# One decoder layer on one core: the first projection's four units side by side by k tiles, constant matmuls in front, a later memory norm and a reordered last product

## The chip, the cores and the metric

The kernel runs on one core of a Trainium2 chip. The metric is the device time of one execution in microseconds. Lower is better. An execution is profiled as well; its trace gives the span from the first to the last instruction and the times of every instruction.

## The reference, cut to what matters

A hybrid decoder layer over 512 positions of width 1024, all in float32:

```
h = rms_norm(x, norm_mix)
hq, hf, hi, hg, mq, mk, mv = split(h @ w_in)          # 4 x 512 and 3 x 512 columns
f = lb + (1 - lb) * sigmoid(hf)                       # HGRN2: q, f, input, gate
x = x + concat(hgrn2(hq, f, hi, hg), moba(mq, mk, mv)) @ w_out
x = x + cross_attention(rms_norm(x, norm_xattn), rms_norm(mem, norm_mem), ...)
x = x + square(relu(rms_norm(x, norm_mlp) @ w_ff1)) @ w_ff2
return rms_norm(x, norm_final)
```

The first projection of this text is `hf`: four heads of 128 columns, contracted over 1024 rows. The memory is `mem`, 256 tokens of width 1024, with a norm of its own (`rstd` is the reciprocal root of its mean square). The last product is the one with `w_ff2`, followed by the residual add and the final norm.

## The kernel before, in words

Every activation is kept transposed, features on the 128 partitions and positions along the free dimension. A contraction over 1024 is eight k tiles of 128. Each float32 operand is split into a high part (rounded to the fp32r type by ScalarE, tile `wh` or `xhi`) and a low part (the remainder, by VectorE, `wl` or `xlo`), and a product is three fp32r matmuls: high by high, high by low, low by high.

Weights come in units of 128 x 1024 float32 (512 KB). A unit is loaded by an SP DMA into a raw tile (`load_unit`, three buffers), split by `split_unit`, and used by the matmuls of `fm_k` or `tm_stage`. `need(u)` is called ahead of unit u and loads up to 6 units and splits up to 2 units ahead of it. Instructions of the head of the kernel and of the MLP run in the order in which the program writes them (`manual_schedule`); each engine works through its own queue in that order.

**The head.** `load_x(k)` loads the eight 256 KB tiles of x, `split_x(k)` splits each with the norm's gain, `square_x(k)` squares it (even k on ScalarE, odd k on VectorE) and VectorE adds the squares to `Sx` and `Sy`. Units 0 to 3 hold one head of `hf` each, all eight k tiles of it side by side. Units 0 and 1 are loaded and split in two parts. The matmuls run for heads 0 and 1 together, k by k, then head 2, then head 3: 4 x 8 x 3 = 96 matmuls of 128 x 512. At `NORM_AT`, behind head 2's k = 6, stand two matmuls with a tile of ones (`nr`) that sum `Sx` over the partitions; ScalarE makes `rb1`, the reciprocal root, out of them (`rsqrt_of`: Ln, then Exp). `ev_f` multiplies the four results by `rb1`. The next stage is `hi` (a `tm_stage`).

**Side work.** Chains of small steps (generators) are put between the matmuls by `pump`. A planner (`Pace`) keeps a model time for each engine; a chain that yields a list of tiles goes on when the model has them ready, and one that yields a number goes on that many model microseconds later. `mem_prep` is such a chain: it loads and splits the memory, sums its squares and calls `norm_rows`, which issues the `nr` matmuls, Ln and Exp (`rbm`), and then transposes `rbm` into a column with small matmuls against the identity (`nc`, result `rcm`). It runs inside the `wo` stage.

**The tail.** The last product runs in seven passes of eight steps (`PLAN`; a step i is one weight unit, 8 k tiles with one 512-column matmul by the high part and one 256-column matmul by the low part). In steps 52 to 55 the outputs are taken in the order `LAST` = 0, 2, 1, 3, and right behind each step's matmuls `ends_last` adds both 256-column halves of the accumulator to the residual (two VectorE adds) and calls `norm_part` (square, scaled copy, sum). `final_half(nb)` sums the squares over partitions with float32 matmuls against ones, takes the reciprocal root, multiplies the half's output in four VectorE pieces and issues one output DMA on SP per piece. Half 0 of the positions is finished during steps 50 and 51; half 1 ends the kernel.

Of the kernel before, what the change touches and what calls it, by code (L numbers as in the profile page):

```python
# [122 lines left out]
def hybrid_layer(ctx: ExitStack, tc: tile.TileContext, xT, memT, ws, vecs, consts, rots, out):  # L123
# [214 lines left out]
    made = {}  # L338
    GAP, SLACK, NORM_AT = 4, 2.5, 6
    since = [0]  # L340
# [119 lines left out]
    def load_x(k):  # L460
        SY.dma_start(xraw[k // 4][:, k % 4, :], xT[:, k])

    A.dma_start(vec, vecs)
    load_x(0)
    load_unit(((0, 2 * P),))
    load_unit(((0, D // 2),))
    load_x(1)
    SY.dma_start(raws[0][:, 2 * P:], ws[0][:, 2 * P:])
    load_x(2)
    SY.dma_start(raws[1][:, D // 2:], ws[1][:, D // 2:])  # L470
    for k in range(3, KT):
        load_x(k)
    nc.gpsimd.memset(eps, EPS)
    nc.gpsimd.memset(ones, 1.0)
    make_identity(nc, ident)
# [27 lines left out]
    def square_x(k):  # L503
        q = sums.get(k) or s2(F32, f"xsq{k}")
        src = xraw[k // 4][:, k % 4, :]
        if k % 2 == 0:
            A.activation(q, src, AF.Square)
        else:
            V.tensor_mul(q, src, src)
        if k not in sums:  # L510
            S, eng = (Sx, V) if k < 4 else (Sy, V)
            eng.tensor_add(S, S, q)
        if k == KT - 1:
            V.tensor_add(Sx, Sx, Sy)

    split_begin()
    split_begin()
    split_x(0)
    split_part(0, 0, 2 * P)
    split_part(1, 0, D // 2)  # L520
    split_x(1)
    split_part(0, 2 * P, D, V)
    split_x(2)
    square_x(0)
    split_x(3)
    split_part(1, D // 2, D, V)
    square_x(1)
    del raws[0], raws[1]
    load_unit()
    load_unit()  # L530
    for k in range(4, KT):
        split_x(k)
        square_x(k - 2)
        if k == 6:
            split_unit(V)
    square_x(KT - 2)
    square_x(KT - 1)
    A.dma_start(cst, consts)
# [7 lines left out]

    def column_sums(ps, src, n, name):

        hi, lo = s2(F32R, f"{name}h"), s2(F32R, f"{name}l")
        A.activation(hi[:, :n], src, AF.Copy)  # L550
        V.tensor_sub(lo[:, :n], src, hi[:, :n].bitcast(F32))
        yield [lo[:, :n]]
        smm(ps[:, :n], ones_r, hi[:, :n], True, False)
        smm(ps[:, :n], ones_r, lo[:, :n], False, True)

    def norm_rows(S, n, dst, cols=None):

        ps = side_bank("nr")
        yield from column_sums(ps, S[:, :n], n, "nr")
        rsqrt_of(dst[:, :n], ps[:, :n], D)  # L560
        if cols is not None:
            yield [dst[:, :n]]
            pc = side_bank("nc")
            for t in range(n // P):
                smm(pc[:, t:t + 1], dst[:, t * P:(t + 1) * P], ident[:, :1])
            V.tensor_copy(cols[:, :n // P], pc[:, :n // P])
# [27 lines left out]

    accs = [acc_bank(f"hf{j}") for j in range(HEADS)]
    for k in range(KT):
        for j in range(2):
            fm_k(j, accs[j], x_act, k, k == 0, k == KT - 1)
    split_unit()
    norm_x = norm_rows(Sx, T, rb1, rc1)  # L600
    next(norm_x)
    for k in range(KT):
        fm_k(2, accs[2], x_act, k, k == 0, k == KT - 1)
        if k == NORM_AT:
            next(norm_x)
    lower_bounds()
    ordered.__exit__(None, None, None)
    need(3)
    for k in range(KT):
        fm_k(3, accs[3], x_act, k, k == 0, k == KT - 1)  # L610
    for h in range(HEADS):
# [228 lines left out]
    def mem_prep():  # L840
# [15 lines left out]
        yield [S[:, :M]]  # L856
        yield from norm_rows(S, M, rbm, rcm)

# [400 lines left out]
    def final_half(nb, S, q):  # L1259

        ps = banks4("Y")[0][:, 0]
        yield [S[:, :half]]
        smm(ps[:, :half], ones, S[:, :half], True, False)
        yield [q[:, :half]]
        smm(ps[:, :half], ones, q[:, :half], False, True)
        r = rbf[:, nb * half:(nb + 1) * half]
        rsqrt_of(r, ps[:, :half], D)
        for eng, a, b in ((V, 0, 2), (V, 2, 4), (V, 4, 7), (V, 7, 8)):
            x = xg(nb, a, b)
            eng.tensor_mul(x, x, r[:, None, :].to_broadcast([P, b - a, half]))  # L1270
            SY.dma_start(out[nb, :, a:b], x)

    def ends(h, t, op):
# [9 lines left out]
    def ends_last(acc, n):  # L1283
        d = x1[0][:, n, half:]
        for x in range(2):
            V.tensor_add(d, d, acc[n // 2][:, n % 2, x * half:(x + 1) * half])
        norm_part(0, 1, n)


# [5 lines left out]
    for p, (name, begins, after) in enumerate(PLAN):  # L1295
# [3 lines left out]
        for j in range(8):  # L1299
# [8 lines left out]
            for k in range(8):  # L1308
                a = ops[4 * p + 2 * c + k // 4][k % 4]
                w_hi, w_lo = hi[:, k * P:(k + 1) * P], lo[:, k * P:(k + 1) * P]  # L1310
                mm(two(acc[n // 2][:, n % 2]), w_hi, a, begins and c == 0 and k == 0, False)
                mm(acc[n // 2][:, n % 2, :half], w_lo, a[:, 0], False, c == 1 and k == 7)
            if c and p < 6:
                rest.append(lambda after=after, acc=acc, n=n: after(acc, n))
            elif c:
                after(acc, n)
    drain(("fin", 0))
# [76 lines left out]
```

## Time and profile before

| | |
|---|---|
| median of 3 runs | 747.05 us (746.96 to 747.32) |
| the profiled execution | 747.39 us |
| its span, first to last instruction | 745.6 us |
| TensorE busy | 728.1 us, 98% of the span |
| VectorE busy | 553.9 us, 74% |
| ScalarE busy | 415.4 us, 56% |
| DMA moved | 136.97 MB, 184 GB/s |

The span is 1.8 us shorter than the time of the same execution. TensorE's busy time counts a matmul from its start to its modelled end, so matmuls that overlap in the pipeline leave no gap. A matmul's row has its start, its duration and, in brackets, the idle time of the engine before it with what ended it. PEld is TensorE's weight load, SPq and ACTq are the DMA issues of SyncE's and ScalarE's queues.

### The profile page before, as it was taken

What the parts mean: (1) busy time and instruction counts of PE and PEld (TensorE: products, weight loads), DVE (VectorE), ACT (ScalarE), POOL (GpSimd) and SP (SyncE); (2) the same over time, 40 slices, a digit from 0 to 9 for tenths busy, and PEclk for the clock granted to TensorE, in tenths of its full rate; (3) what the DMA queues carried; (4) which work ended last, traced back from release to release, by engine and by line L of the source; (5) the groups of instructions that cost most, each with busy time, mean ns of one, the idle gap of its engine ahead of it and who ended that gap; (6) DMA issues with size and microseconds to landing.
All of it is one profiled execution on the core that took longest, in us unless ns stands there. A gap on an engine that the chain in (4) does not pass through costs nothing.

```text
span 745.6 us, 11110 instructions
## 1 busy us (share of the span) xinstructions
PE 728.1 (98%) x4248; PEld 636.2 (85%) x4248; DVE 553.9 (74%) x907; ACT 415.4 (56%) x634; POOL 49.5 (7%) x62
## 2 busy tenths in 40 slices
PE   6999999999999999999999999999999999999995
PEld 4888888777777898888888999999999888888884
DVE  5888554877766655777468788787888899987875
ACT  6673357434855454455356655555556654547662
POOL 1000000000011110012001011132110000000000
PEclk9999999999999999999999999999999999999998
DMA  8425334544589898459836398889995655546622
GB/s 277 144 84 165 116 113 123 167 136 138 163 200 251 204 271 326 142 117 259 280 113 151 98 254 217 232 197 237 244 225 204 211 185 193 174 163 205 198 91 79
DMA packets 44438, 136.97 MB, mean 184 GB/s; under 512 B 4545, under 2 KB 6977, under 8 KB 43745
## 3 DMA queue, kind: packets, MB, share of 16 engines
q1 hardware_dynamic: 34944, 110.64, 43.4%
q0 software_dynamic: 8960, 25.17, 19.0%
q8 instruction: 33, 0.54, 0.3%
q10 hardware_dynamic: 480, 0.45, 0.2%
q14 instruction: 21, 0.16, 0.1%
HBM read 134.15 MB, written 35.65 MB: 228 GB/s over the span
## 4 chain that ended last, share of the span: by engine, by line
PE 94%; DVE 2%; DMA 1%; ACT 1%; issue 1%; DVEq 0%; ACTq 0%
PE X L115 23%; PE Y L115 19%; PE xo L115 7%; PE mkq L115 6%; PE xq L115 6%; PE wo L115 5%; PE hg L115 3%; PE mv L115 3%; PE memv L115 3%; PE hq L115 3%; PE hi L115 3%; PE memk L115 2%; PE hf L115 2%; PE xs L115 2%; PE a L115 1%; PE sc L115 1%
## 5 line engine op out<-in xcount | busy, mean ns | idle before, releaser
L115 ACT ACTIVATE wh<-wr 128x1024 fp32r<-128x1024 f32 (+2 forms) x126 | 130.3, 1041 | 118.8 <-PE wo L115 19.6
L115 DVE TENSOR_TENSOR wl<-wr,wh 128x1024 fp32r<-128x1024 f32 (+2 forms) x126 | 151.2, 1204 | 33.6 <-ACT wh L115 23.3
L115 PE MATMUL X<-op,wh 128*128 128x512 f32 x256 | 90.6, 398 | 0.3 <-DVE x L115 0.3
L115 PE MATMUL X<-op,wl 128*128 128x256 f32 x256 | 72.3, 283 | 0.0
L115 PE MATMUL Y<-op,wh 128*128 128x512 f32 x192 | 68.0, 399 | 0.0
L115 PEld LDWEIGHTS X<-op,wh 128*128 128x128 f32 x256 | 48.1, 188 | 12.1 <-issue 0.5
L115 PE MATMUL Y<-op,wl 128*128 128x256 f32 x192 | 53.9, 281 | 0.0
L200 POOL DMA_DIRECT2D u<-in_ws_dram x32 | 31.0, 968 | 328.7 <-PE hg L115 201.3
L115 PEld LDWEIGHTS X<-op,wl 128*128 128x128 f32 x256 | 48.4, 189 | 0.3 <-DVE wl L115 0.2
L115 PE MATMUL Y<-OS,wh 128*128 128x256 f32 x256 | 47.2, 284 | 0.2 <-ACT t L115 0.2
L115 PE MATMUL X<-OS,wh 128*128 128x256 f32 x256 | 46.5, 283 | 0.0
L115 PEld LDWEIGHTS Y<-op,wh 128*128 128x128 f32 x192 | 36.1, 188 | 9.0
L115 PEld LDWEIGHTS Y<-OS,wh 128*128 128x128 f32 x256 | 39.9, 192 | 0.5 <-ACT t L115 0.4
L115 PEld LDWEIGHTS X<-OS,wh 128*128 128x128 f32 x256 | 39.9, 192 | 0.0
L115 PEld LDWEIGHTS Y<-op,wl 128*128 128x128 f32 x192 | 36.3, 189 | 0.0
L115 PE MATMUL X<-OS,wl 128*128 128x256 f32 x128 | 36.2, 283 | 0.0
L115 PE MATMUL Y<-OS,wl 128*128 128x256 f32 x128 | 36.2, 283 | 0.0
L115 ACT ACTIVATE g<-t 128x512 f32<-128x512 f32 x32 | 19.0, 625 | 30.2 <-DVE t L115 30.2
L115 DVE TENSOR_TENSOR op<-g,op 128x1024 fp32r<-128x1024 f32 x24 | 29.3, 1220 | 2.8 <-ACT op L115 2.8
L115 ACT ACTIVATE op<-g 128x1024 fp32r<-128x1024 f32 x28 | 29.2, 1044 | 0.5 <-PE X L115 0.5
L115 ACT ACT_TABLE_LOAD x22 | 28.2, 1283 | 1.6 <-PEq L1382 1.2
L115 PE MATMUL mkq<-xhi,wh 128*128 128x512 f32 x64 | 26.7, 417 | 0.0
(307 smaller groups left out, 2028.8 us busy)
## 6 DMA issues: line engine op xcount, KB each, us to landing
wr<-in_ws_dram SPq DMA_DIRECT2D x90, 512.0 KB, 4.4
u<-in_ws_dram POOLq DMA_DIRECT2D x32, 512.0 KB, 7.6
wr<-u SPq DMA_DIRECT2D x32, 512.0 KB, 3.3
u<-in_ws_dram SPq DMA_DIRECT2D x16, 512.0 KB, 4.1
u<-u SPq DMA_DIRECT2D x16, 512.0 KB, 5.3
wA<-in_ws_dram SPq DMA_DIRECT2D x8, 512.0 KB, 5.6
wD<-in_ws_dram SPq DMA_DIRECT2D x8, 512.0 KB, 6.7
wB<-in_ws_dram SPq DMA_DIRECT2D x8, 512.0 KB, 3.6
```

The costliest lines, as they stand in the source:

```text
L115: return f(*args, **kw)
L200: return nc.gpsimd.dma_start(dst, src, accum_op=ALU.add, max_dma_last_dim=4 * D)
```

## The change

1. The four units of `hf` are cut the other way: raw tile v holds k tiles 2v and 2v + 1 of all four heads (`load_first`, `split_first`). The loop over k is outermost, with the four heads inside it; two of the four accumulators come from the side pool. Unit 0 arrives in three DMAs (two of them on ScalarE's queue), units 1 to 3 in one each; `vec` moves to SP's queue, ahead of the first x tile.
2. All eight squares of x are made by ScalarE, and the last ones come behind all splits. `nr` stands in front of k = 7.
3. `WARM` = 11 float32 matmuls of the tile of ones with itself (128 x 128) stand in front of the head's matmuls; their result is not used. The memset of the ones comes first on GpSimd.
4. In `mem_prep`, `norm_rows` waits 3.0 model microseconds more ahead of its `nr` matmuls and again ahead of its `nc` matmuls.
5. In the tail, what follows steps 52 to 54 is put off to the next step, behind that step's weight split (`rest`). In step 55 the high-part matmul is cut into two of 256 columns that add both halves of the operand into the lower half of the accumulator, so its upper half is complete earlier: `low_last` adds it behind step 53, and one add is left at the end. `final_half(0)` yields 6.0 model microseconds behind each of its pieces.

```diff
-    A.dma_start(vec, vecs)
+    def load_first(v, k=None, h=slice(None), eng=None):
+        ...
+        src = ws[h if h != slice(None) else slice(0, HEADS)].rearrange("h p c -> p h c")
+        if k is None:
+            (eng or SY).dma_start(raws[v].rearrange("p (h c) -> p h c", h=HEADS), src[:, :, 2 * v * P:(2 * v + 2) * P])
+        else:
+            (eng or SY).dma_start(by_k(raws[v])[:, h, k], src[:, :, (2 * v + k) * P:(2 * v + k + 1) * P])
+
+    def split_first(v, k, h=slice(None)):
+        hi, lo, raw = (by_k(t)[:, h, k] for t in (his[v], los[v], raws[v]))
+        A.activation(hi, raw, AF.Copy)
+        V.tensor_sub(lo, raw, hi.bitcast(F32))
+
+    SY.dma_start(vec, vecs)
     load_x(0)
-    load_unit(((0, 2 * P),))
-    load_unit(((0, D // 2),))
+    load_first(0, 0, slice(0, 2), A)
+    load_first(0, 0, slice(2, 4), A)
     load_x(1)
-    SY.dma_start(raws[0][:, 2 * P:], ws[0][:, 2 * P:])
+    load_first(0, 1)
     load_x(2)
-    SY.dma_start(raws[1][:, D // 2:], ws[1][:, D // 2:])
-    for k in range(3, KT):
+    load_first(1)
+    load_x(3)
+    load_x(4)
+    load_first(2)
+    for k in range(5, KT):
         load_x(k)
+    nc.gpsimd.memset(ones, 1.0)
     nc.gpsimd.memset(eps, EPS)
-    nc.gpsimd.memset(ones, 1.0)
...
-        if k % 2 == 0:
-            A.activation(q, src, AF.Square)
-        else:
-            V.tensor_mul(q, src, src)
+        A.activation(q, src, AF.Square)
...
+    warm = side_bank("warm")
+    for i in range(WARM):
+        PE.matmul(warm[:, :P], ones, ones, start=True, stop=True, skip_group_check=True)
+
     split_begin()
-    split_begin()
+    split_first(0, 0, slice(0, 2))
     split_x(0)
-    split_part(0, 0, 2 * P)
-    split_part(1, 0, D // 2)
+    split_first(0, 0, slice(2, 4))
     split_x(1)
-    split_part(0, 2 * P, D, V)
+    split_first(0, 1)
+    load_first(3)
     split_x(2)
+    split_unit()
     square_x(0)
     split_x(3)
-    split_part(1, D // 2, D, V)
     square_x(1)
...
+    split_x(4)
+    split_unit()
+    square_x(2)
+    split_x(5)
+    square_x(3)
+    split_x(6)
+    split_unit()
+    square_x(4)
+    split_x(7)
+    for k in range(5, KT):
+        square_x(k)
...
         yield [lo[:, :n]]
+        if later:
+            yield later
         smm(ps[:, :n], ones_r, hi[:, :n], True, False)
...
             yield [dst[:, :n]]
+            if later:
+                yield later
             pc = side_bank("nc")
...
-    accs = [acc_bank(f"hf{j}") for j in range(HEADS)]
-    for k in range(KT):
-        for j in range(2):
-            fm_k(j, accs[j], x_act, k, k == 0, k == KT - 1)
-    split_unit()
+    accs = [(acc_bank if j < 2 else side_bank)(f"hf{j}") for j in range(HEADS)]
     norm_x = norm_rows(Sx, T, rb1, rc1)
     next(norm_x)
     for k in range(KT):
-        fm_k(2, accs[2], x_act, k, k == 0, k == KT - 1)
-        if k == NORM_AT:
+        if k % 2 == 0:
+            need(k // 2)
+        if k == KT - 1:
             next(norm_x)
-    lower_bounds()
-    ordered.__exit__(None, None, None)
-    need(3)
-    for k in range(KT):
-        fm_k(3, accs[3], x_act, k, k == 0, k == KT - 1)
+            lower_bounds()
+            ordered.__exit__(None, None, None)
+        a_hi, a_lo = x_act(k)
+        for hs in ((0, 1), (2, 3)) if k == 0 else ((0,), (1,), (2,), (3,)):
+            w = {h: [by_k(t[k // 2])[:, h, k % 2] for t in (his, los)] for h in hs}
+            for h in hs:
+                mm(accs[h], w[h][0], a_hi, k == 0, False)
+            for h in hs:
+                mm(accs[h], w[h][1], a_hi, False, False)
+            for h in hs:
+                mm(accs[h], w[h][0], a_lo, False, k == KT - 1)
...
-        yield from norm_rows(S, M, rbm, rcm)
+        yield from norm_rows(S, M, rbm, rcm, 3.0)
...
             SY.dma_start(out[nb, :, a:b], x)
+            if not nb:
+                yield 6.0
...
-        for x in range(2):
+        for x in range(1 if n == LAST[3] else 2):
...
+    def low_last(acc, n):
+        d = x1[0][:, n, half:]
+        V.tensor_add(d, d, acc[n // 2][:, n % 2, half:])
...
-                mm(two(acc[n // 2][:, n % 2]), w_hi, a, begins and c == 0 and k == 0, False)
+                if i == 55:
+                    for x in range(2):
+                        mm(acc[n // 2][:, n % 2, :half], w_hi, a[:, x], False, False)
+                else:
+                    mm(two(acc[n // 2][:, n % 2]), w_hi, a, begins and c == 0 and k == 0, False)
...
-            if c and p < 6:
+            if i == 55:
+                after(acc, n)
+            elif c:
                 rest.append(lambda after=after, acc=acc, n=n: after(acc, n))
-            elif c:
-                after(acc, n)
+            if i == 53:
+                rest.append(lambda acc=acc: low_last(acc, LAST[3]))
```

## Rows read from the trace of the kernel before

**Rows 1.** Busy time by stage; the last columns are clock, DMA share, GB/s.

```profile
9.90:32.80 22.90, 21.68 (x92) 16.59 (x91) 21.21 (x36) 16.56 (x24) 0.00 (x0) 1.00 0.64 214
33.00:100.00 67.00, 67.00 (x344) 57.20 (x342) 51.00 (x141) 35.11 (x48) 0.00 (x0) 1.00 0.36 118
...
206.00:257.00 51.00, 49.90 (x231) 40.68 (x230) 33.41 (x48) 27.73 (x39) 7.33 (x9) 1.00 0.87 219
...
712.00:745.60 33.60, 24.85 (x136) 20.64 (x135) 22.14 (x32) 14.50 (x25) 0.00 (x0) 0.92 0.24 79
```

**Rows 2.** Chain that ended last: start, duration, engine, tile, instructions.

```profile
5.05 5.82 DMA xraw<-in_xT_dram
...
82.91 1.56 PE ho L115 x14
...
210.05 20.02 PE wo L115 x88
...
438.03 8.64 PE Y L115 x72
```

**Rows 3.** The page's costliest groups: the weight splits (busy, mean ns).

```profile
L115 ACT ACTIVATE wh<-wr 128x1024 fp32r<-128x1024 f32 (+2 forms) x126 | 130.3, 1041 | 118.8 <-PE wo L115 19.6
L115 DVE TENSOR_TENSOR wl<-wr,wh 128x1024 fp32r<-128x1024 f32 (+2 forms) x126 | 151.2, 1204 | 33.6 <-ACT wh L115 23.3
```

**Rows 4.** Timeline of the head: ScalarE's first instructions, TensorE's matmuls.

```profile
1.18 1.28 ACT L115 ACT_TABLE_LOAD   x1 [1.18 <-PEq L1382]
...
5.06 0.72 ACT L115 ACTIVATE xhi<-xraw,vec 128x512 fp32r<-128x512 f32 x1 [2.38 <-DMA vec<-in_vecs_dram]
...
6.14 0.79 PE L115 MATMUL hf<-xhi,wh 128*128 128x512 f32 x1 [6.14 <-ACT wh L115]
...
9.89 0.39 PE L115 MATMUL hf<-xhi,wl 128*128 128x512 f32 x1
...
32.78 0.39 PE L115 MATMUL hi<-wh,xhi 128*128 128x512 f32 x1
```

**Rows 5.** DMA issues from 3.0 to 3.4 us: count, size, us to landing.

```profile
xraw<-in_xT_dram SPq DMA_DIRECT2D x1, 256.0 KB, 6.4
```

**Rows 6.** SP's queue at that DMA: start, duration.

```profile
3.07 0.43 SPq L115 DMA_DIRECT2D xraw<-in_xT_dram  x1
```

**Rows 7.** DMA queues, 723 to 746 us: packets, MB, share of 16 engines.

```profile
q1 hardware_dynamic: 2176, 2.10, 26.5%
```

**Rows 8.** Timeline inside `wo`: the memory's norm.

```profile
234.46 0.39 PE L115 MATMUL wo<-mixlo,wh 128*128 128x512 f32 x1
...
235.49 0.42 ACT L115 ACTIVATE rbm<-rbm 128x256 f32<-128x256 f32 x1
...
235.95 0.61 PE L115 MATMUL nc<-ident,rbm 128*128 128x1 f32 x4 [1.10 <-ACT rbm L115]
```

**Rows 9.** Timeline of the tail: VectorE and TensorE.

```profile
723.43 2.49 DVE L115 TENSOR_TENSOR g<-g,rb 128x512 f32<-128x512 f32 x4
725.84 2.35 DVE L115 TENSOR_TENSOR wl<-wr,wh 128x1024 fp32r<-128x1024 f32 x2
...
731.95 0.87 DVE L115 TENSOR_TENSOR x<-x,X 128x256 f32<-128x256 f32 x2
...
732.43 0.28 PE L115 MATMUL X<-op,wl 128*128 128x256 f32 x1
732.96 0.47 PE L115 MATMUL X<-op,wh 128*128 128x512 f32 x1 [0.25 <-DVE x L115]
...
735.70 0.28 PE L115 MATMUL X<-op,wl 128*128 128x256 f32 x1
...
736.01 0.88 DVE L115 TENSOR_TENSOR x<-x,X 128x256 f32<-128x256 f32 x2 [0.59 <-PE X L115]
...
739.08 2.50 DVE L115 TENSOR_TENSOR g<-g,rb 128x512 f32<-128x512 f32 x4 [2.19 <-ACT rb L115]
```

**Rows 10.** Waits of TensorE's weight loads from 710 us: total, times, longest.

```profile
PEld X L115 <- DVE wl L115: 0.2, 1, 0.2
```

More of the change, by code (lines that the diff above doesn't have):

```diff
@@ L338, in hybrid_layer @@
     made = {}
-    GAP, SLACK, NORM_AT = 4, 2.5, 6
+    GAP, SLACK, WARM = 4, 2.5, 11
     since = [0]
@@ L461, in load_x, with by_k @@
         SY.dma_start(xraw[k // 4][:, k % 4, :], xT[:, k])
-    A.dma_start(vec, vecs)
+    def by_k(t):
+        return t.rearrange("p (h k c) -> p h k c", h=HEADS, k=2)
+    def load_first(v, k=None, h=slice(None), eng=None):
+        if v not in raws:
+            raws[v] = raw_tile(f"wr{v}", False)
+            state["load"] += 1
+        src = ws[h if h != slice(None) else slice(0, HEADS)].rearrange("h p c -> p h c")
[8 more added lines that the diff above has]
+    SY.dma_start(vec, vecs)
     load_x(0)
-    load_unit(((0, 2 * P),))
-    load_unit(((0, D // 2),))
+    load_first(0, 0, slice(0, 2), A)
+    load_first(0, 0, slice(2, 4), A)
     load_x(1)
-    SY.dma_start(raws[0][:, 2 * P:], ws[0][:, 2 * P:])
+    load_first(0, 1)
     load_x(2)
-    SY.dma_start(raws[1][:, D // 2:], ws[1][:, D // 2:])
-    for k in range(3, KT):
+    load_first(1)
[3 more added lines that the diff above has]
+    for k in range(5, KT):
         load_x(k)
+    nc.gpsimd.memset(ones, 1.0)
     nc.gpsimd.memset(eps, EPS)
-    nc.gpsimd.memset(ones, 1.0)
     make_identity(nc, ident)
@@ L514, in square_x @@
             V.tensor_add(Sx, Sx, Sy)
+    warm = side_bank("warm")
+    for i in range(WARM):
+        PE.matmul(warm[:, :P], ones, ones, start=True, stop=True, skip_group_check=True)
     split_begin()
-    split_begin()
+    split_first(0, 0, slice(0, 2))
     split_x(0)
-    split_part(0, 0, 2 * P)
-    split_part(1, 0, D // 2)
+    split_first(0, 0, slice(2, 4))
     split_x(1)
-    split_part(0, 2 * P, D, V)
+    split_first(0, 1)
+    load_first(3)
     split_x(2)
+    split_unit()
     square_x(0)
     split_x(3)
-    split_part(1, D // 2, D, V)
     square_x(1)
[L528 to L537, printed above, removed]
+    split_x(4)
[9 more added lines that the diff above has]
+        square_x(k)
+    del raws[0]
     A.dma_start(cst, consts)
@@ L545, in rsqrt_of, with column_sums @@
         A.activation(dst, dst, AF.Exp, scale=-0.5)
-    def column_sums(ps, src, n, name):
+    def column_sums(ps, src, n, name, later=None):
         hi, lo = s2(F32R, f"{name}h"), s2(F32R, f"{name}l")
@@ L552, in column_sums, with norm_rows @@
         yield [lo[:, :n]]
+        if later:
+            yield later
         smm(ps[:, :n], ones_r, hi[:, :n], True, False)
         smm(ps[:, :n], ones_r, lo[:, :n], False, True)
-    def norm_rows(S, n, dst, cols=None):
+    def norm_rows(S, n, dst, cols=None, later=None):
         ps = side_bank("nr")
-        yield from column_sums(ps, S[:, :n], n, "nr")
+        yield from column_sums(ps, S[:, :n], n, "nr", later)
         rsqrt_of(dst[:, :n], ps[:, :n], D)
```

## The prediction, written before the changed kernel ran

> **What bounds the kernel now.** I read the page first (TensorE is busy 98% of the span), then the busy times by stage, then the chain of waits, then the timelines of the places where TensorE isn't busy. The stages say where time can be had. From 33 to 100 us TensorE is busy for all 67.00 us, and so it is nearly everywhere up to 712 us; the stage with `wo` lacks 1.1 us of 51, the tail from 712 us lacks 8.75 of 33.6 [rows 1]. In the head TensorE looks 95% busy, but only because overlapping matmuls leave no gap: VectorE is busy 21.21 of 22.90 us there, and that engine sets the pace [rows 1]. So the kernel is bound by TensorE in its middle, which the change leaves alone, and by something else at three places, and the change is about just these: the head, the memory's norm, the tail.
>
> For the size of a matmul I use the chain: 88 matmuls of 512 columns in 20.02 us, 0.2275 us each, when nothing is late [rows 2].
>
> **The head, before.** From the first matmul at 6.14 us to the first one of `hi` at 32.78 us pass 26.64 us [rows 4]. It holds 96 matmuls and the two `nr`: 98 x 0.2275 = 22.3 us. So 4.35 us are lost. Nine matmuls start between 6.14 and 9.89 us, 0.417 us each: 512 columns in that time are the lower of the two clock levels, 1.2 GHz, and TensorE had done nothing before [rows 4]. Against 9 x 0.2275 = 2.05 this costs 1.7 us. The other 2.65 us are waits for splits.
>
> **The head, after.** Three things decide: when the first operands are there, whether each k tile's operands come faster than TensorE uses them, and the clock.
>
> *First operands.* Before, ScalarE starts on x at 5.06 us, when `vec` has landed [rows 4]. Now x's tile is issued one SP issue (0.43 us [rows 6]) later, behind `vec`, and two 128 KB weight pieces share the DMA engines. I take 5.5 us for `xhi`; the weight half comes first and is off the path. 5.5 + 0.72 and a small step: first matmul at 6.3 us. Bounds: 5.8 us (x as early as before) and 7.4 us (below).
>
> *Landing.* Take x's third tile: issued at 3.07 us, 6.4 us to landing, so 9.47 us, with 1562 KB asked for up to it [rows 5, 6] (26 + 256 + 128 + 256 + 256 + 384 + 256, by the order in the code). x's fourth tile lands at 10.87 us, with 2074 KB [rows 2]. That is a line of 366 KB per us. On it, the new order has 538 KB up to x's first tile with all of k = 0 (6.67 us, hence the bound of 6.67 + 0.72 = 7.4), 1050 KB up to unit 0's k = 1 (8.07 us) and 1818 KB up to unit 1 (10.17 us).
>
> *Short packets.* Unit 0 moves in runs of 512 bytes, 1024 packets. Nothing before shows their price. The output's runs of 1 KB do for one end: 2176 packets took 26.5% of 16 engines for 23 us, 45 ns each [rows 7], and 1 KB at 366 KB per us over 16 engines is 45 ns as well. So a packet of 512 bytes costs between 22 ns (its bytes) and 45 ns (no less than 1 KB); nothing extra, or up to 1024 x 23 / 16 = 1.45 us in all. As 1 KB shows hardly a fixed part, I take 30 ns, 0.5 us. k = 1 of unit 0 lands at 8.6 us, unit 1 at 10.7 us. The Trainium skill's page DMA: Bandwidth & Descriptors, Specifications, gives 512 B as the least transfer for line rate. By it the 0.5 us would be nothing and the head 0.3 us shorter than below; no row here has such runs alone.
>
> *The walk.* k = 0: 6.3 + 12 x 0.2275 = 9.03 us. A split of 1024 columns takes 1.04 us on ScalarE and 1.20 on VectorE [rows 3]; one of 512 I put at 0.7 on each, half and a start. k = 1 has ScalarE's behind 8.6, so 9.3, and VectorE's, 10.0, where 9.53 was wanted: 0.27 + 0.47 lost, end at 12.5 us. k = 2 needs unit 1: 10.7 + 1.04 + 1.20 = 12.95 us for the low part, wanted at 12.73: 0.2 lost, end at 15.4 us. From there a k takes 2.73 us on TensorE; VectorE has three operations of 512 columns in it (x tile, half a unit, add), about 0.6 each, half of 1.20, and ScalarE as many; nothing is late. Five k and the two `nr`: 14.1 us. `hi` begins at 29.5 us instead of 32.78: **-3.3 us**.
>
> *What is moved with it.* Four squares go from VectorE, which set the pace, to ScalarE, which was busy 16.56 of 22.90 us [rows 1]: 4 x 0.6 us fit, and without that slack they would cost 2.4. `nr` needs all squares before k = 7; VectorE has 8 x 0.6 + 4 x 1.2 + 8 x 0.6 = 14.4 us of work (x tiles, units, adds and the remainder for `nr`) from 6 us on, so it is done near 22 with its waits, and k = 7 starts near 26.3. `rb1` is now ready only at the end of the head, but nobody on TensorE waits: `hi`'s third accumulator needs `hf`'s bank 12 matmuls later. Unit 3's load waits on SP until unit 0's raw tile is free (10.0 us); behind it queue only the loads of units 4 to 6, wanted from 29.5 us on. ScalarE's two DMA issues stand before its table load, with nothing due before 5 us.
>
> *The constants.* Eleven float32 matmuls of 128 x 128: the chain has 14 passes, 7 such matmuls, in 1.56 us at the upper clock, 0.223 each [rows 2]; twice that at 1.2 GHz is 4.9 us. The engines' queues start at 1.2 us [rows 4], so they end by 6.1 us, before the operands are there: cost nothing. If the clock rises under them, the 1.7 us are saved, and the walk above holds; if not, the first nine real matmuls take 1.7 us more, of which 0.8 is waiting already. With that and the late bound of 7.4 us the head gains 1.4 us; with 5.8 us and no waits, 4.7 us.
>
> **The memory's norm.** TensorE would have gone on at 234.69 us (234.46 + 0.2275) but starts `nc` at 235.95, as `rbm` ends at 235.91 [rows 8]: 1.1 to 1.26 us. The change gives the chain 3 model us more ahead of `nr` and again between `nr` and `nc`; the planner counts 0.215 us for a matmul of 0.2275, so that is 3.2 us, against the 1.26 that were missing. The stage goes on for 20 us more, so nothing waits for `rcm`. **-1.1 us**, bounds 0 (Ln and Exp meet other ScalarE work at the new place) and 1.3.
>
> **The tail.** In step 55 the first matmul starts at 732.96 us, behind the add at 731.95 + 0.87, though the one before it began at 732.43 and holds TensorE for 0.12 [rows 9]: 0.41 us. In the changed order unit 55's split no longer queues behind step 52's ScalarE work, and half 0's four output multiplies, 2.49 us in one lump [rows 9], are spread, so VectorE is earlier with all that follows; the 0.2 us wait for a weight's low part goes too [rows 10]. At the end one VectorE add of two goes: 0.87 / 2 = 0.43 us, on the chain. Against it: step 55 has 24 matmuls of 256 columns at 8.64 / 72 = 0.12 [rows 2], 2.88 us, where it took 735.70 + 0.12 - 732.96 = 2.86: nothing. Put-off pieces of half 0 fall into VectorE's 2.19 us of idle time before its last multiplies [rows 9]; without that cover the last would cost 0.4. VectorE's queue from 723.43 to the end of the matmuls (three splits of 1.2, seven adds of 0.43, three sums with their waits, three of the four pieces of 2.49) adds up to some 11 of 11.8 us, so the margin is under 1 us. **-1.0 us**, bounds -0.4 and -1.3.
>
> **Sum.** 3.3 + 1.1 + 1.0 = 5.4 us. The profiled execution took 747.39 us, 1.8 more than its span, and 0.34 over the median of 747.05; the span becomes 740.2. I count from the median: **741.6 us**.
>
> **Rivals.**
> *The head is fed late or at the low clock.* For: no row shows such short runs or float32 matmuls raising the clock. Against: 1 KB runs at full rate. Head 1.4, all else as above: 3.5 us, 743.5 us.
> *The head runs without a wait.* 4.7 + 1.1 + 1.2: 740.0 us. Against: at 9.47 us the line is only at 1562 KB.
> *Given back in the middle.* The planner's model times behind the head change, and with them the places of side steps. One misplaced step cost 1.1 us [rows 8]; two more of that kind make 743.8 us, three 744.9. Against: in 67 us with many such steps TensorE lacks nothing [rows 1].
> *Slower: the constants hold TensorE.* Place: before the first real matmul. At c us each, TensorE is free at 1.2 + 11c; from c = 0.46 on each 0.1 costs 1.1 us, at 0.95 the whole gain is gone, at 1.1 the kernel takes 748.7 us. Against: 0.223 at the upper clock.
> *The head change does nothing* because VectorE still sets the pace: only 1.1 + 1.0, 745 us. Against: its work per k, 1.8 us, is under TensorE's 2.73.
>
> **Numbers.** A run here tells a difference from 0.2%, 1.5 us. Forecast (740.6 to 742.8) 0.55; late feed 0.17; no wait 0.10; given back 0.10; nothing in the head 0.04; constants 0.04. Range: from the bound 4.7 + 1.3 + 1.3 = 7.3 us, 739.7, rounded down to 739.5, to 744.6; above it lie half of the given-back case and the last two. Faster by over 0.2%: 0.92; within: 0.05; slower: 0.03.
>
> **What would show it.** Right: `hf`'s second matmul 0.23 us after its first; `hi` starting near 29.5 us; gaps only in k = 1 and 2; no idle time before `nc` in `wo`; step 55 starting 0.12 us after step 54's last matmul; one add between the last matmul and the last square. Wrong: matmuls of `hf` 0.42 us apart, the constants ending behind 6.3 us, unit 1 landing behind 11.5 us, new waits of TensorE between 33 and 700 us.

## The result, and the profile after

The changed kernel takes 740.74 us (median of 6 runs, 740.62 to 741.21). The kernel before, run beside it, took 747.18 us, so 6.44 us are saved: ratio 0.9915, interval 0.9902 to 0.9928. 741.6 was forecast. The profiled execution's span fell from 745.6 to 738.9 us.

Busy time by stage after the change, over the stretches that answer to [rows 1] (head; 67 us of the middle; `wo`). Columns: window, length, then PE, PEld, DVE, ACT and POOL busy with counts, clock, DMA share, GB/s.

```profile
5.70:28.60 22.90, 22.76 (x98) 18.43 (x99) 19.03 (x27) 18.58 (x28) 0.00 (x0) 1.00 0.79 257
28.70:95.70 67.00, 67.00 (x344) 57.21 (x343) 53.11 (x148) 38.71 (x53) 0.00 (x0) 1.00 0.37 124
202.00:248.70 46.70, 46.70 (x208) 38.11 (x207) 30.92 (x45) 25.28 (x36) 6.51 (x8) 1.00 0.90 226
```

The first window now holds the whole head, 98 matmuls; before, a window as long held 92 [rows 1]. VectorE is busy 19.03 us and ScalarE 18.58, where it was 21.21 and 16.56: neither sets the pace. `wo` has no idle time left. The middle is as full as it was.

Timeline of the head after, the answer to [rows 4]: start, duration, engine, instruction, in brackets the idle time before it.

```profile
0.99 4.27 PE L115 MATMUL warm<-ones 128*128 128x128 f32 x22 [0.99 <-POOL eps L496]
...
4.95 0.72 ACT L115 ACTIVATE xhi<-xraw,vec 128x512 fp32r<-128x512 f32 x1 [1.25 <-DMA xraw<-in_xT_dram]
...
5.73 0.74 PE L115 MATMUL hf<-xhi,wh 128*128 128x512 f32 x2 [0.47 <-ACT xhi L115]
...
9.47 1.06 ACT L115 ACTIVATE wh<-wr 128x1024 fp32r<-128x1024 f32 x1 [1.24 <-DMA wr<-in_ws_dram]
...
10.57 1.23 DVE L115 TENSOR_TENSOR wl<-wr,wh 128x1024 fp32r<-128x1024 f32 x1 [1.55 <-ACT wh L115]
...
11.34 0.39 PE L115 MATMUL hf<-xhi,wh 128*128 128x512 f32 x1
11.85 0.50 PE L115 MATMUL hf<-xhi,wl 128*128 128x512 f32 x1
...
12.18 0.39 PE L115 MATMUL hf<-xlo,wh 128*128 128x512 f32 x1
...
28.61 0.39 PE L115 MATMUL hi<-wh,xhi 128*128 128x512 f32 x1
```

The constants are done at 5.26 us, `xhi` begins at 4.95 and the first matmul starts at 5.73; from the second on matmuls follow each other at 0.23 us. k = 1 doesn't wait. k = 2 does: unit 1's low part begins at 10.57 and takes 1.23, and from 11.34 to 12.18 pass 0.84 us where two matmuls take 0.455, so the wait costs 0.38. `hi` starts at 28.61 instead of 32.78: **4.17 us** from the head. Some 0.3 us of that is the execution's own: the runs e4, e6 and e7, which have the same head, start `hi` at 28.33 to 28.39, and e3, which has the head of before, at 32.41.

Timeline inside `wo` after, the answer to [rows 8]:

```profile
202.14 0.39 PE L115 MATMUL wo<-mixhi,wh 128*128 128x512 f32 x1
...
226.63 0.29 PE L115 MATMUL nr<-nrh,ones_r 128*128 128x256 f32 x1
...
226.76 0.28 PE L115 MATMUL nr<-nrl,ones_r 128*128 128x256 f32 x1
...
231.49 0.42 ACT L115 ACTIVATE rbm<-rbm 128x256 f32<-128x256 f32 x1
...
238.01 0.50 PE L115 MATMUL nc<-ident,rbm 128*128 128x1 f32 x4
...
248.71 0.28 PE L115 MATMUL memk<-mhi,wh 128*128 128x256 f32 x1
```

`rbm` is done 6.1 us ahead of `nc`, and neither `nr` nor `nc` shows idle time. From the first `wo` matmul to the first of the next stage, `memk`, pass 46.57 us instead of 48.10 (254.44 - 206.34): **1.53 us**.

The tail after, the answer to [rows 9]:

```profile
706.12 0.40 PE L115 MATMUL X<-op,wh 128*128 128x512 f32 x1
...
725.87 0.42 DVE L115 TENSOR_TENSOR x<-x,X 128x256 f32<-128x256 f32 x1
...
726.51 0.28 PE L115 MATMUL X<-op,wl 128*128 128x256 f32 x1
726.62 0.40 PE L115 MATMUL X<-op,wh 128*128 128x256 f32 x2
...
729.37 0.28 PE L115 MATMUL X<-op,wl 128*128 128x256 f32 x1
...
729.69 0.42 DVE L115 TENSOR_TENSOR x<-x,X 128x256 f32<-128x256 f32 x1 [0.84 <-PE X L115]
```

Step 55's first matmul starts at 726.62, 0.11 us behind the start of step 54's last. `low_last` has run at 725.87, so one add of 0.42 us is left behind the last matmul. The last pass begins at 706.12 (711.84 before) and the last of its matmuls at 729.37 (735.70 before): 23.25 instead of 23.86 us. From there to the end of the span it is 9.53 instead of 9.88. The last pass's first matmul in the kernel before:

```profile
711.84 0.40 PE L115 MATMUL X<-op,wh 128*128 128x512 f32 x1
```

That makes **0.96 us** from the tail. 4.17 + 1.53 + 0.96 = 6.66, and the spans differ by 6.68; nothing was given back between.

### The profile page after: what moved, and what is told of

Its sections match the earlier page's. It is cut to its first block, busy times and chain, and to the rows that moved or that the text cites. A ratio compares the mean times of both kernels' runs of the same rounds, so it can differ in the third digit from the quotient of the medians.

```text
span 738.9 us, 11173 instructions
## 1 busy us (share of the span) xinstructions
PE 729.0 (99%) x4278; PEld 640.4 (87%) x4278; DVE 551.5 (75%) x903; ACT 417.5 (56%) x638; POOL 49.4 (7%) x62
## 4 chain that ended last, share of the span: by engine, by line
PE 97%; DMA 1%; DVE 1%; ACT 1%; issue 0%; SPq 0%; DVEq 0%; ACTq 0%
PE X L115 25%; PE Y L115 19%; PE xo L115 7%; PE mkq L115 6%; PE xq L115 6%; PE wo L115 6%; PE hg L115 3%; PE mv L115 3%; PE memv L115 3%; PE hq L115 3%; PE hi L115 3%; PE memk L115 3%; PE hf L115 2%; PE xs L115 2%; PE a L115 1%; PE po L115 1%
## 5 line engine op out<-in xcount | busy, mean ns | idle before, releaser
L115 PE MATMUL X<-op,wh 128*128 128x512 f32 (+1 forms) x264 | 90.5, 391 | 0.0
```

The lines of the kernel that those rows point to most:

```text
L115: return f(*args, **kw)
```

## The experiments

The kernel before ran beside every one; "saved" is its median there (747.04 to 747.22 us) less that of the run, and the last column is that against the 6.44 us of the changed kernel. A ratio's interval is about 0.13% to either side, 1 us, so differences under that rest on the traces.

| run | median us (range) | ratio | saved | against 6.44 |
|---|---|---|---|---|
| e1_no_constants | 742.98 (742.72 to 743.17) | 0.9945 | 4.18 | -2.26 |
| e2_constants_only | 746.94 (746.69 to 747.88) | 0.9999 | 0.22 | |
| e3_memory_only | 745.63 (745.24 to 745.83) | 0.9978 | 1.53 | |
| e4_old_tail | 742.12 (741.24 to 742.48) | 0.9932 | 5.04 | -1.40 |
| e5_squares_shared | 741.24 (741.16 to 741.34) | 0.9922 | 5.80 | -0.64 |
| e6_one_lump | 741.30 (741.22 to 741.93) | 0.9926 | 5.74 | -0.70 |
| e7_two_adds | 741.09 (740.86 to 741.28) | 0.9920 | 5.95 | -0.49 |
| e8_constants_22 | 742.92 (741.95 to 743.15) | 0.9942 | 4.12 | -2.32 |
| e9_load_order | 742.16 (741.71 to 742.71) | 0.9935 | 4.91 | -1.53 |
| e10_unit0_whole | 741.36 (741.18 to 741.50) | 0.9924 | 5.71 | -0.73 |
| e11_unit1_halves | 740.22 (740.15 to 740.29) | 0.9906 | 7.00 | +0.56 |
| e12_late_half | 741.02 (740.76 to 741.24) | 0.9916 | 6.20 | -0.24 |

### The constants: taken out, alone, doubled

e1 is the changed kernel without them, e2 the kernel before with them alone, e8 the changed kernel with 22.

```diff
-    for i in range(WARM):                                      # e1
-        PE.matmul(warm[:, :P], ones, ones, ...)
-    nc.gpsimd.memset(ones, 1.0)                                # e2, on the kernel before:
+    nc.gpsimd.memset(ones, 1.0)                                # now ahead of eps
+    for i in range(11):
+        PE.matmul(warm[:, :P], ones, ones, ...)
-    GAP, SLACK, WARM = 4, 2.5, 11                              # e8
+    GAP, SLACK, WARM = 4, 2.5, 22
```

> The changed kernel without the eleven constant matmuls. Theory (the constants raise the clock ahead of the real work): the first matmuls of hf run 0.42 us apart for some 3.7 us, which costs 1.7 us, of which the 0.5 us wait in k = 2 is covered: 1.2 us slower than the changed kernel, about 741.9 us. Rival (the clock rises by itself by the time the operands are there, the layout is everything): 740.7 us, matmuls of hf 0.23 us apart from the first.

> The kernel before with the eleven constant matmuls in front and nothing else. Theory (in the old head VectorE's remainders of x set the times at which TensorE can go on, the last of them at 20.1 us): TensorE only waits longer for them, gain under 0.3 us, 746.9 to 747.2 us, hi still begins near 32.8 us. Rival (the clock is worth 1.7 us in either layout): 745.5 us.

> The changed kernel with 22 matmuls of constants instead of 11. In the changed kernel their 22 passes run 0.99 to 5.26 us, 0.388 us a matmul, and the first matmul of `hf` starts at 5.73 us. Theory (their price is low until they end behind the first operands, then their duration at the clock of the moment counts): the next eleven run at the upper clock, 0.223 us each, so they end at 5.26 + 2.45 = 7.7 us, the first matmul of `hf` starts 2.0 us later, the 0.5 us wait for unit 1 is covered by it; 742.2 to 742.7 us. Rival (they go on at 0.39 to 0.45 us each): they end near 9.5 to 10 us, 744.0 to 745.0 us. If neither shows (no matmul delayed), 740.7 us.

TensorE's timeline in e1:

```profile
5.73 1.22 PE L115 MATMUL hf<-xhi,wh 128*128 128x512 f32 x2 [5.73 <-ACT xhi L115]
...
11.01 0.63 PE L115 MATMUL hf<-xhi,wh 128*128 128x512 f32 x1
```

The first matmul starts at the same 5.73 us, but the first twelve take 11.01 - 5.73 = 5.28 us, 0.44 each: the lower level, 1.2 GHz, after a TensorE that had done nothing. At 0.2275 they would take 2.73, so 2.55 us are lost; the wait of 0.38 us in k = 2 of the changed kernel is covered by it, `hi` starts 2.32 us later (30.93), and the medians differ by 2.26. The theory's 741.9 was too low because it priced nine slow matmuls, as before the change [rows 4].

In e2, the kernel before with constants, the waits of the first 40 us (engine, tile, releaser: total us, times, longest):

```profile
PEld hf L115 <- DVE xlo L115: 3.8, 6, 1.0
```

There the first matmuls run at the upper clock and then wait for VectorE's low parts: 0.22 us saved, and the ratio's interval (0.9989 to 1.0008) includes no change. The constants pay only in the new order, where operands come as fast as TensorE takes them. The start of `hi` tells the same: 32.78 us before, 30.93 with the new order alone (e1), 32.34 with the constants alone (32.41 in e3, which has the head of before without them), 28.61 with both, which is more than the two gains added.

TensorE in e8, microsecond by microsecond (window, length, busy and instructions, clock, DMA share, GB/s):

```profile
6.00:7.00 1.00, 1.00 (x7) 1.00 0.86 246
7.00:8.00 1.00, 1.00 (x11) 1.00 1.01 313
```

and its timeline:

```profile
0.99 8.04 PE L115 MATMUL warm<-ones 128*128 128x128 f32 x44 [0.99 <-POOL eps L496]
8.78 0.71 PE L115 MATMUL hf<-xhi,wh 128*128 128x512 f32 x2
```

Until 7 us six or seven passes stand in a microsecond, the lower level, and then eleven, the upper one. So the second eleven didn't run at 0.223 us each, as the theory had it, nor all at the rival's 0.39 to 0.45, but some at either. The first real matmul starts 3.05 us later, no later wait is left, and 2.32 us less are saved, nearer the theory's 742.7 than the rival's 744, and in neither range. That is the mechanism of the prediction's slower rival, met at 22 constants: once they outlast the operands, they hold TensorE.

### The squares

```diff
-        A.activation(q, src, AF.Square)
+        if k % 2 == 0:
+            A.activation(q, src, AF.Square)
+        else:
+            V.tensor_mul(q, src, src)
```

> The changed kernel with the four odd squares of x back on VectorE. Theory (the new order feeds TensorE in any case, the offload is not what pays): in the changed kernel's head TensorE waits once, 0.5 us, for the low part of unit 1; the squares stand behind the splits of the k tiles that TensorE uses next, so 4 x 0.6 us more on VectorE fill idle time. `hi` starts 0 to 0.3 us later than at 28.61 us; 740.7 to 741.0 us. Rival (taking the squares off VectorE, which set the pace before, is what pays): VectorE falls behind by up to 4 x 0.6 us, waits of `hf` for low parts of 1.5 to 2.4 us appear, `hi` starts near 30.5 us, 742.5 to 743 us.

A wait of TensorE in e5's first 60 us:

```profile
PEld nr L115 <- DVE nrl L115: 0.5, 1, 0.5
```

The changed kernel has no such wait. No matmul of `hf` waits for a low part, as the theory said, but the sum of the squares ends later and `nr`, which stands ahead of k = 7, waits for its low part. The offload is worth some 0.6 us, through `nr`, and not the 2.4 us of work that it moves. In this profile `hi` starts at 29.11, 0.50 later: the first matmul came 0.21 later, ahead of the edit; k = 2 didn't wait, which gives 0.38 back; and around `nr` 0.67 us more pass than in the changed kernel.

### The memory's norm alone

```diff
+        if later:
+            yield later                # ahead of nr, and again ahead of nc
-        yield from norm_rows(S, M, rbm, rcm)
+        yield from norm_rows(S, M, rbm, rcm, 3.0)
```

> The kernel before with the memory norm's two waits of 3.0 and nothing else. Theory: the idle time before nc goes and the matmuls around nr close up, 1.3 to 1.5 us faster, 745.7 us; nothing changes before wo. Rival (the 1.5 us between wo and memk in the changed kernel came from another order of side steps behind the new head): under 0.5 us.

1.53 us in the medians, and the stage takes 46.53 us where it took 48.10. The timeline of the kernel before has the part that [rows 8] left out:

```profile
206.34 0.39 PE L115 MATMUL wo<-mixhi,wh 128*128 128x512 f32 x1
...
229.68 0.39 PE L115 MATMUL wo<-mixhi,wh 128*128 128x512 f32 x1
...
230.01 0.19 PEld L115 LDWEIGHTS nr<-nrh,ones_r 128*128 128x128 f32 x1 [0.36 <-ACT nrh L115]
...
236.42 0.48 PE L115 MATMUL wo<-mixhi,wl 128*128 128x512 f32 x1
...
254.44 0.28 PE L115 MATMUL memk<-mhi,wh 128*128 128x256 f32 x1
```

The first `nr` waits for `nrh`: it starts 0.33 us behind the matmul in front of it and the next follows it 0.22 later, where the changed kernel needs 0.23 and 0.12. That is 0.2 us. (The two `nr` start 0.69 us apart in the kernel before and 0.13 in the changed one, but two `wo` matmuls stand between them before, so that difference isn't lost time.) The greater part is `nc`: from the `wo` matmul in front of it [rows 8] to the one behind it pass 236.42 - 234.46 = 1.96 us, and 0.59 in the changed kernel, 1.37 less. The delay cures `nr` as well as `nc`; the two add up to 1.56, within 0.03 of what the stage gains.

### The tail: all of it undone, one lump, two adds

e4 has the whole tail of the kernel before, e6 only the multiplies of half 0 in one lump, e7 only step 55 in 512-column matmuls with both adds at the end.

```diff
-            if not nb:                                          # e6 (and e4)
-                yield 6.0
-        for x in range(1 if n == LAST[3] else 2):               # e7 (and e4)
+        for x in range(2):
-                if i == 55:
-                    for x in range(2):
-                        mm(acc[n // 2][:, n % 2, :half], w_hi, a[:, x], False, False)
-            if i == 53:
-                rest.append(lambda acc=acc: low_last(acc, LAST[3]))
-            if i == 55:                                         # e4 alone
-                after(acc, n)
-            elif c:
+            if c and p < 6:
                 rest.append(lambda after=after, acc=acc, n=n: after(acc, n))
+            elif c:
+                after(acc, n)
```

> The changed kernel with the tail of the kernel before. Theory: 1.0 us slower than the changed kernel, 741.7 us, and the stall before step 55 (0.4 us) and the second add at the end (0.43 us) are back. Rival (with the head 4 us earlier, the tail's waits fall elsewhere): under 0.4 us.

> The changed kernel with the four output multiplies of half 0 in one lump again. Theory (the last product's last pass runs without a wait because VectorE's work is spread): a lump of 2.5 us on VectorE between steps 52 and 54 delays a weight split behind it, TensorE waits 0.2 to 0.5 us in the last pass; 741.0 to 741.2 us. Rival (the put-off sums alone cure the wait before step 55): no wait, 740.7 us, and the last X matmul starts 23.4 us after the last pass as before.

> The changed kernel with step 55 in 512-column matmuls again, so both halves of the last accumulator are added behind the last matmul. Theory (the two adds lie on the chain that ends the kernel): from the last matmul of the last product to the end of the span 0.43 us more, 741.2 us; the last pass itself as long as before. Rival (ScalarE's sum chain behind the adds has slack, or the 24 short matmuls of step 55 cost what the add saves): 740.7 us.

e4's profiled execution took 742.48 us, the top of its range. Its tail has the wait of before again (`X` for VectorE's `x`, 0.3 us) and is 1.1 us longer. Its head is 0.2 us shorter, and 0.9 us are lost in the MLP near 556 us; there a late transfer stands in the chain that neither the changed kernel's chain nor that of before has:

```profile
534.48 12.96 DMA wB<-in_ws_dram
```

So the tail's 1.0 holds in this execution, and why that transfer was late is open. The median's 1.40 holds some of both.

VectorE and TensorE in e6:

```profile
717.42 2.49 DVE L115 TENSOR_TENSOR g<-g,rb 128x512 f32<-128x512 f32 x4
...
721.10 0.19 PEld L115 LDWEIGHTS X<-op,wl 128*128 128x128 f32 x1 [0.25 <-DVE wl L115]
...
724.24 0.47 PE L115 MATMUL X<-op,wh 128*128 128x512 f32 x1 [0.29 <-DVE x L115]
```

The lump makes two waits: for a weight's low part, and, as the adds queue behind it, for the accumulator, in front of step 54. The last pass of this profile is 0.93 us longer than the changed kernel's, and the median shows 0.70; both are over the theory's upper end of 0.5. The put-off sums alone don't cure the tail; the spread multiplies are needed with them. Whether the spread multiplies alone would do it was not run.

VectorE in e7:

```profile
729.42 0.88 DVE L115 TENSOR_TENSOR x<-x,X 128x256 f32<-128x256 f32 x2 [0.98 <-PE X L115]
```

Two adds instead of one, and from the last matmul (729.11) to the end of the span it is 9.95 us instead of 9.53: 0.42, the duration of an add, on the chain. The median shows 0.49. Step 55 itself takes 2.66 us at the starts (726.45 to 729.11) and 2.75 in the changed kernel, so the short matmuls cost 0.09 us of what the add saves.

### Loading and splitting the first operands

```diff
-    SY.dma_start(vec, vecs)                                    # e9
     load_x(0)
+    SY.dma_start(vec, vecs)
...
-    load_x(2)
     load_first(1)
+    load_x(2)
-    load_first(0, 0, slice(0, 2), A)                           # e10
-    load_first(0, 0, slice(2, 4), A)
+    load_first(0, None, slice(None), A)
     load_x(1)
-    load_first(0, 1)
     split_x(2)                                                 # e11
-    split_unit()
+    split_begin()
+    split_first(1, 0)
+    split_first(1, 1)
+    del raws[1]
+    load_first(0, 0, slice(0, 2), A)                           # e12, on e11
     SY.dma_start(vec, vecs)
     load_x(0)
-    load_first(0, 0, slice(0, 2), A)
-    load_first(0, 0, slice(2, 4), A)
+    load_first(0, 0, slice(2, 4))
-    GAP, SLACK, WARM = 4, 2.5, 11
+    GAP, SLACK, WARM = 4, 2.5, 9
```

> The changed kernel with two pairs of loads exchanged on SP's queue: x's first tile ahead of `vec`, and unit 1 ahead of x's third tile. Theory (what is left in the head is set by when the first operands land, then by unit 1): `xhi` starts one issue, 0.4 us, earlier, so the first matmul of `hf` is bound by the constants and the weight half, near 5.3 to 5.5 us instead of 5.7 to 5.9; the low part of unit 1 is ready before k = 2, so the 0.5 us wait of the changed kernel's profile is gone; 739.8 to 740.4 us. Rival (the constants, which end at 5.26 us, and `vec`, now later, set the start; x's third tile, now later, makes the wait that unit 1 made): 740.6 to 741.2 us.

> The changed kernel with unit 0 in one DMA of 512 KB on ScalarE's queue, in runs of 1 KB, instead of three DMAs in runs of 512 bytes. Theory (early bytes decide: 256 KB more stand ahead of k = 0's operands; at 300 to 340 GB/s that is 0.8 us, and short runs cost little): the first matmul of `hf` starts at 6.4 to 6.8 us, k = 1 doesn't wait, `hi` starts 0.5 to 0.9 us later; 741.2 to 741.7 us. Rival (runs of 512 bytes are dear, by up to 1.45 us in all): what is lost at the start is won back by faster landing, 740.4 to 740.9 us.

> The changed kernel with unit 1's split cut in two, k = 2 ahead of k = 3. Theory (the wait of 0.5 us in k = 2 is for a low part of 1024 columns of which only half is wanted yet): the low part of k = 2 is ready at 9.47 + 0.63 + 0.69 = 10.8 us, ahead of 11.57 where it is wanted, no wait is left in the head, `hi` starts 22.4 to 22.5 us after the first matmul of `hf` instead of 22.88; 740.2 to 740.5 us (other profiles of this head had no such wait, so the median gains less than 0.5). Rival (two starts more on each engine push the splits behind it late): 740.7 to 741.2 us.

> The kernel of the run before, with the second half of k = 0's weights issued on SP behind x's first tile and not ahead of it, and nine constants instead of eleven. Theory (the start is bound by the bytes ahead of x's first tile): 128 of 538 KB fewer stand ahead of it, at 250 to 340 GB/s 0.4 to 0.5 us, `xhi` starts at 4.5 us, the constants end by 4.9 us, the first matmul of `hf` starts at 5.2 to 5.3 us; 739.8 to 740.2 us. Rival (all early DMAs share the engines, so x's first tile lands as before, or the second half is then late in k = 0, or the clock rises later behind fewer constants): 740.5 to 741.5 us, and the profile shows which.

ScalarE and VectorE in e9:

```profile
5.03 0.71 ACT L115 ACTIVATE xhi<-xraw,vec 128x512 fp32r<-128x512 f32 x1
...
7.97 0.63 ACT L115 ACTIVATE wh<-wr 128x512 fp32r<-128x512 f32 x1 [1.31 <-DMA wr<-in_ws_dram]
...
10.74 1.04 ACT L115 ACTIVATE wh<-wr 128x1024 fp32r<-128x1024 f32 x1
...
11.81 1.23 DVE L115 TENSOR_TENSOR wl<-wr,wh 128x1024 fp32r<-128x1024 f32 x1 [0.20 <-ACT wh L115]
```

e9 went worse than its rival. Its first loads, issued at 0.73, 0.73 and 1.18 us in the order of these rows (the last column is us to landing):

```profile
xraw<-in_xT_dram SPq DMA_DIRECT2D x1, 256.0 KB, 3.5
wr<-in_ws_dram ACTq DMA_DIRECT2D x1, 128.0 KB, 4.0
vec<-in_vecs_dram SPq DMA_DIRECT2D x1, 26.0 KB, 3.7
```

x's first tile, issued 0.45 us earlier, lands at 4.2 us and not at 4.9 as in the changed kernel. But the first weights, split ahead of it, now land at 4.7 (3.3 in the changed kernel) and `vec` at 4.9 (2.8), so `xhi` begins at 5.03 all the same and the first matmul starts at 5.79. The rival said this of `vec`. k = 1's weights are split at 7.97, not 6.83 as in the changed kernel, although both are issued at 2.1 us with the same bytes ahead of them; behind them now stands a 512 KB unit and not a 256 KB tile. And x's third tile, now loaded behind unit 1 but still split ahead of it, holds unit 1's split on ScalarE until 10.74, though unit 1 was issued earlier: its low part begins at 11.81 instead of 10.57. The order of loads has to agree with the order of splits.

e10's first matmul:

```profile
6.79 0.73 PE L115 MATMUL hf<-xhi,wh 128*128 128x512 f32 x2 [0.74 <-ACT xhi L115]
```

1.06 us later than in the changed kernel; then no matmul of the head waits, `hi` starts at 29.22 (+0.61). The median is 741.36, as the theory had it: what comes ahead of the first operands is what costs. The short runs cost little: the head takes 22.43 us from its first matmul here, and 22.49 and 22.47 in e6 and e7, which load as the changed kernel does and had no wait in k = 2.

In e11, TensorE's first matmul and unit 1's split in two:

```profile
5.32 0.73 PE L115 MATMUL hf<-xhi,wh 128*128 128x512 f32 x2 [0.17 <-ACT xhi L115]
...
10.11 1.29 DVE L115 TENSOR_TENSOR wl<-wr,wh 128x512 fp32r<-128x512 f32 x2 [0.63 <-ACT wh L115]
```

The first low part starts at 10.11 and is done ahead of k = 2; the wait is gone, `hi` starts at 27.93, and the head takes 22.61 us from its first matmul instead of 22.88. 740.22 us is the best of all kernels here; its range and the changed kernel's don't overlap, but the two intervals do. That its first matmul came 0.4 us earlier isn't the edit's doing: it stands ahead of it. Nor does the wait that the edit takes away come in every execution: e6 and e7, with unit 1 uncut, had none, as unit 1 landed at 9.1 to 9.2 us there and not at 9.4 to 9.5 as in the changed kernel and in e11. And 0.3 us are lost again in this profile's `wo`, which takes 46.90 us. So what is shown of the edit is that it takes away a wait worth 0.38 us where that comes.

In e12 the start is early too, 5.17 us, but k = 1 pays:

```profile
8.65 0.49 PE L115 MATMUL hf<-xhi,wh 128*128 128x512 f32 x1 [0.43 <-ACT wh L115]
```

One DMA more on SP puts every later one an issue back; k = 1's weights are issued at 2.64 us, not 2.12 as in e11, land 0.95 us later and are split at 7.97, and `hi` starts at 28.87. The issue explains half of that; between 4 and 7 us the DMA engines also move less than in e11 (224 against 300 GB/s), and why is open. The median lies in the rival's range, by a way that the rival didn't name: k = 0 has its second half in time, and k = 1 is late.

## Why the prediction was right, and where its numbers were off

**What bounds, and where.** Right: all 6.66 us come from the three places named, and the middle has none of them. "Given back in the middle" didn't come. "The head change does nothing" fell too.

**The head: 3.3 forecast, 4.17 measured.** The mechanism held, the term mis-sized is the landing, and part of the size is luck. Forecast: first matmul 6.3, k = 1 at 8.6, unit 1 at 10.7 us. The transfers as issued (KB each, median us from issue to landing, first 12 us after the change):

```profile
wr<-in_ws_dram ACTq DMA_DIRECT2D x2, 128.0 KB, 3.3
xraw<-in_xT_dram SPq DMA_DIRECT2D x1, 256.0 KB, 3.7
wr<-in_ws_dram SPq DMA_DIRECT2D x1, 256.0 KB, 4.7
```

x's first tile is issued at 1.18 us with 3.7 us to landing (4.9), k = 1 of unit 0 at 2.11 and lands at 6.8, and ScalarE starts on unit 1 at 9.47. All three are 0.55 to 1.8 us early. So the first matmul came 0.57 us sooner (6.3 to 5.73), and instead of 0.94 us of waiting in k = 1 and 2 there was 0.38, in k = 2 alone. That makes 1.13 us; 0.24 go again, as the matmuls start a little over 0.2275 us apart, at the first ones above all (the first twelve take 2.89 us, not 2.73), and 0.89 are left, by which `hi` is early (29.5 to 28.61).

Two terms failed in this. The first is x's first tile. The 5.06 us of before, to which one issue was added, was the landing of `vec`; the tile itself was there at 4.85 (4.1 us from its issue at 0.74), and after the change, issued 0.44 us later, it landed at the same time. How early it lands is partly luck: in the eight profiles that load alike (the changed kernel, e1, e4 to e8, e11) `xhi` begins at 4.55 to 5.16 us, all ahead of the 5.5 taken. The second is the line of 366 KB per us, for k = 1 and unit 1. It was laid through two late tiles of before and counted only the bytes asked for up to each. The DMA rate in the kernel before (window, length, TensorE, clock, share, GB/s) tells why it needn't hold earlier:

```profile
3.00:4.00 1.00, 0.00 (x0) 1.00 0.50 159
...
8.00:9.00 1.00, 1.00 (x4) 1.00 1.05 405
```

Added up to 9.47 us some 2,200 KB had moved there where the line counts 1,562: later transfers share the engines with the one that is waited for, the more of them the later it is. In the first microseconds few do, so early tiles land sooner than a line through late ones says. The changed kernel moves 730 KB by 4.9 us, with 538 asked for up to x's first tile. That the difference of both counts is the other transfers' share is worked out, not measured apart; e9 bears it out: there the same transfer, issued at the same time with the same bytes ahead of it, landed 1.1 us later, with the first two loads exchanged ahead of it and a larger one behind it. On top of the line stood 0.5 us for short packets, of which some 0.3 were due.

**Short packets.** The queue of ScalarE after the change (packets, MB, share of 16 engines in 12 us) carries runs of 512 bytes almost alone:

```profile
q10 hardware_dynamic: 544, 0.26, 7.5%
```

0.075 x 16 x 12 / 544 = 26.5 ns a packet, between the bounds of 22 and 45 and near the 30 taken. The Trainium skill's page DMA: Bandwidth & Descriptors, Specifications, which gives 512 B as the least transfer for line rate, is nearly borne out: 26.5 against 22 ns. e10 agrees, since whole runs won nothing. Two corrections to the prediction: by its own walk, nothing for short packets would have made the head 0.5 us shorter, not 0.3 (no loss in k = 1, 0.4 in k = 2). And a price did stand in the trace of before: the load of `cmask` moves 128 packets of 512 bytes from 16.7 to 18.4 us, 27 ns each in the median.

**The constants.** "End by 6.1, cost nothing, save 1.7": in the profiled execution they end at 5.26, cost nothing, and save 2.26 (e1). The slow period that they replace isn't of a fixed size: it took 3.75 us before [rows 4], and 5.28 in e1, so the 1.7 was too small. The pass rate showed that the clock rises under them. In the profiles of e5, e7, e9 and e10 it doesn't rise before their last pass, which starts at 5.63 us; `hf` then starts at the upper level behind them all the same. As `xhi` is done between 5.27 and 5.88 us in the profiles that load alike, eleven leave hardly any margin when the clock rises that late, and 22 cost 2.3 us (e8): the slower rival is real.

**The moved squares.** They fit ScalarE, as forecast; putting them back costs 0.64 us through `nr`, not through the splits (e5).

**The memory: 1.1 forecast, bounds 0 and 1.3; 1.53 measured (e3 alone: 1.53).** This lies above the upper bound. The step took the lesser of its two readings of `nc`'s wait, 1.1 to 1.26, where the whole detour costs 1.37; and the late `nrh` in front of `nr`, 0.2 us, was in the trace too and was not counted.

**The tail: 1.0 forecast, 0.96 measured.** Each term is there: the wait before step 55 (gone; e4 has it again, and e6's lump makes one like it before step 54), the add (0.42, e7), and 24 short matmuls for almost nothing (726.62 to 729.37 is 2.75 us at the starts, 2.74 before [rows 9], 2.66 in e7 with the long ones and no wait ahead). VectorE's margin under 1 us was real: from 717.72 to 729.50 us it is busy for 9.52 of 11.78 us and waits three times 0.48 for ScalarE's squares. The lump is the same work at another place, and it breaks the last pass (e6).

## What to carry to other kernels

At the start of a kernel, order the loads by who is waited for first, split them in that same order, and price a landing from early rows and from what else is in flight, not from a line through late ones. A load put first pays only if all that the first step needs comes first with it (e9). Matmuls of constants ahead of the first operands pay only where the operands then come as fast as TensorE takes them, and only as long as they end first. When a wait of a chain is read from one row, look at the chain's earlier links too: the same delay may cure several.

## What was not expected of the hardware

The moment at which TensorE passes from its lower to its upper level differs between executions that begin alike. TensorE's first instructions are the same in the changed kernel and in e8: passes of the constants go from seven to eleven a microsecond between 4 and 5 us in the one, and only at 7 us in the other. By the starts of the passes the change comes at 4.2 us in e11, 4.4 in the changed kernel and e4, 4.9 in e6 and 7.2 in e8; in e5, e7, e9 and e10 no pass is at the upper level up to the last, at 5.63, and the first matmuls of `hf` right behind are. In all these windows the granted clock reads 1.00 throughout, so it is the rate of the passes that shows the level there, not that column.

An earlier issue of one load isn't an earlier start: in e9 x's first tile landed 0.6 us sooner, the weights and `vec`, which the first split needs as well, 1.4 and 2.1 us later. And 128 KB fewer ahead of x's first tile did little against an execution's own spread (e12: `xhi` at 4.39, e11 without that edit: 4.55, all profiles that load alike: 4.55 to 5.16).
